# The mixer's u and merge gates z as five steps of seven products, with weight sums in DRAM, and i and v ahead of u

## Chip, cores, metric

The kernel runs on one core of a Trainium2 chip (trn2). The metric is the device time of one execution in microseconds. A core has a matrix engine (TensorE, "PE" in the profile; "PEld" is its loading of weights), VectorE (DVE), ScalarE (ACT), GpSimd (POOL) and SyncE (SP); DMA transfers go through queues that SP (q1 in the profile) and POOL (q0) fill, and are carried out by 16 DMA engines. Matrix products add up in PSUM, which has 8 banks of 128 x 512 f32.

## The reference, cut to what matters

Two layers act on x of 512 tokens x 1024 (ALPHA, BETA and norms as in the code): a feed-forward half step, the mixer, another feed-forward half step, each followed by a layer norm. What this case touches is the mixer's input projection and what uses its parts:

```python
zq, zf, zi, zg, zu, zv, za, zb = jnp.split(x @ w_in, IN_SPLITS, axis=-1)   # 512 each for the first six, 1024 for za and zb
...
o = hgrn2_chunkwise(q, k, i, log_f)                     # 4 heads; normalized per head, times silu(zg)
y_a = o @ w_branch_a
u = jax.nn.gelu(zu)
v = layer_norm(jax.nn.gelu(zv), sg_ln_g, sg_ln_b)
mixed = jnp.einsum('gts,bnsgc->bntgc', ws, v) + sg_bs.T[None, None, :, :, None]
y_b = (u * mixed.reshape(B, T, SG_WIDTH)) @ w_branch_b
y = jax.nn.sigmoid(za) * y_a + jax.nn.sigmoid(zb) * y_b
return y @ w_out
```

All is f32. The inputs x and all weights come from DRAM.

## The kernel before, in words

**Precision.** A product of f32 matrices is made as three passes of a faster type: each operand is split into a high part "h" (an ACT conversion) and a low part "l" (a DVE subtraction, `split`, L125 to L127), and high x high, high x low and low x high are added. The activations x are kept split and transposed as xh and xl: four tiles of 128 features x 2 x 512 tokens. `weights` (L129 to L137) loads a block of 128 x 1024 weights (512 KB) by SP into one of NRAW = 4 raw buffers and splits it into two of NW = 10 tiles, so five blocks can stand ready.

**The blocks of features.** `features` (L790) multiplies one block, 128 output features of all 1024 inputs, by all 512 tokens: `proj` (L147, matmul L155) does 8 k-tiles x 3 passes = 24 matmuls of 512 columns into one bank. So are made f and q (8 blocks), g (4 blocks), u (4 blocks, L1060 to L1063, evicted by ACT with the gelu) and z, that is za and zb (16 blocks, L1109 to L1113, evicted by ACT with the sigmoid).

**Seven products.** i and v are made otherwise, in `two_tokens` (L797): x is cut into halves of the tokens and of the features, the weights likewise, and the four block products of each result are made by seven products (the Strassen-Winograd scheme), whose operands are sums. The sums of x, called s1 to s4, are made and split by `x_sums` (L499) as a side task. The sums of the weights (t13, which holds two, t2 and t4) are made in DRAM by POOL's DMAs, `sums_in_dram` (L294): a copy of one quarter, then a DMA that adds another quarter to it, in the order t13, t2, t4, where each needs the one before. Four steps of w_iv have 8.4 MB of this traffic. The FFN works by seven products too, with 256 columns in each matmul (`seven_pairs` L572, matmul L590), the tokens being cut in two.

**The order of work.** The code is one stream. `Flow` (L50 to L80) is a planner with an estimated clock: `tick` is called after each group of matmuls, adds their estimated time and lets the side task that is due do its next step; `finish` runs a task to its end. A task yields the delay to its next step. SUM_GAP = 7000 ns is the delay between the DMA groups of the sums. In the mixer the stream is: f/q blocks with the sums of x and of w_iv as side tasks (L1034, L1035); g; u; `finish` of both tasks; `two_tokens`; the norm of v (L1075 to L1087, whose scale and shift are in sgp, whose reciprocal root is POOL's `vr`, and whose mixing weights and bias are in cst); z, with two side tasks: `head_out` (L983) of each head in turn, and `spatial` (L1091), the mixing matmuls `mx` and, on DVE, `mv` and the splits `sg`; then the branch projections y and the output projection.

`head_out` makes on PE the transposes `kt`, the state `st`, the outputs `o` (L1009); then ACT squares, DVE sums (`ms`, L1013), POOL makes the reciprocal root `rs` (L186, L187), DVE scales (`on`, L1016), PE transposes back (`ot`, L1021), and DVE and ACT make `ov` and `og`. Every engine carries out its own instructions in their order, so one that waits holds up all behind it.

Of the kernel before, what the change touches and what calls it, by code (L numbers as in the profile page):

```python
# [28 lines left out]
F32 = mybir.dt.float32  # L29
# [6 lines left out]
P = 128  # L36
# [47 lines left out]
def trunk(ctx: ExitStack, tc, x_in, xt_in, w13, w2, w_in, w_iv, w_br, w_out, ln_g, ln_b, lb_in, hgn, sgg, sgb, sgws,  # L84
# [414 lines left out]
    def x_sums(s, gap=X_GAP):  # L499
# [21 lines left out]
        parts("s3")  # L521
        for q in range(2):
            V.tensor_tensor(v["s2"][q], firsts[q], v["s1"][q], op=ALU.subtract)
        yield 0.0, gap
        parts("s2")
        for q in range(2):
            V.tensor_tensor(v["s4"][q], v["s4"][q], v["s2"][q], op=ALU.subtract)
        yield 0.0, gap
        parts("s4")
# [219 lines left out]

    def gates():  # L750
# [28 lines left out]
    def mixer(l, lb, om, first, next_weights):  # L779
# [7 lines left out]
        blk = iter(range(4, 32))  # L787
# [9 lines left out]
        def two_tokens():  # L797
# [3 lines left out]
            for k in ks:  # L801
                for name, q, ts in (("A11", k // 2, lo_t), ("A12", 2 + k // 2, lo_t), ("A22", 2 + k // 2, hi_t)):
                    ops[name, k] = xh[q][:, k % 2, ts], xl[q][:, k % 2, ts]
                for name in ("s1", "s2", "s3", "s4"):
                    ops[name, k] = s[name][0][:, k], s[name][1][:, k]
            s.clear()
# [8 lines left out]
            for ps, p in ((A, P1), (B, P6), (C, P5)):  # L815
                for tt in range(2):
# [3 lines left out]
                    elif ps is B:  # L820
                        V.tensor_tensor(u[:, tt], u[:, tt], B[tt], op=ALU.subtract)
                    else:
                        S.activation(p5[:, tt], C[tt], AF.Copy)
            for k in ks:
                for c in ("A11", "s1", "s2"):
                    del ops[c, k]
# [21 lines left out]


# [133 lines left out]
        def head_out(h):  # L983
# [13 lines left out]
            state = gate[h][:, 0, 0:P]  # L997
# [36 lines left out]
        s_task = flow.add(x_sums(s, 6000.0), 2000.0)  # L1034
        in_dram = flow.add(seven.sums_in_dram(seven.order, 4), 12000.0)  # L1035
# [31 lines left out]
        late.append(flow.add(all_out(), 4000.0))  # L1067
        cst = slot("cst")
# [145 lines left out]
def _layout(x, ffn1_w13, ffn1_w2, ffn2_w13, ffn2_w2, ln_g, ln_b, w_in, hg_lb, hg_norm_g, sg_ln_g, sg_ln_b,  # L1214
# [25 lines left out]
    blocks += [feat(16 + j) for j in range(4)]  # L1240
    blocks += [feat(24 + j) for j in range(16)]
# [4 lines left out]
        "x": c(x), "xt": c(np.asarray(x)[0].T.reshape(4, 2, P, T).transpose(0, 2, 1, 3)).reshape(4, P, D), "w13": w13, "w2": w2, "w_in": np.stack(blocks, 1), "w_iv": quarters(iv, KT // 2),  # L1246
# [12 lines left out]
_INS = ["x", "xt", "w13", "w2", "w_in", "w_iv", "w_br", "w_out", "ln_g", "ln_b", "lb", "hgn", "sgg", "sgb", "sgws",  # L1259
# [26 lines left out]
```

## Time and profile before

| what | value |
|---|---|
| time, median of 3 runs | 2036.38 us (2035.0 to 2036.6) |
| profiled execution, its span | 2033.5 us; the median lies 2.9 us above it |
| TensorE busy | 2022.2 us, 99% |
| VectorE, ScalarE, GpSimd busy | 1639.4 (81%), 996.8 (49%), 370.5 us (18%) |
| mean granted TensorE clock | 0.998 |
| first layer: u starts, i and v start, z starts | 430.1, 453.2, 491.3 us |
| second layer: u starts, i and v start | 1440.7, 1463.8 us |
| matmul of 512 columns, of 256 columns, length | 0.39 to 0.40, 0.28 us |

The rows of a timeline give start, length, engine, line, operation, what is written "<-" what is read, and the number of instructions. Matmuls overlap in the pipeline, so a length is longer than the distance to the next start. A row of waits names the waiting engine, tile and line, then what it waited for, and the total, the number and the longest in us. In groups, "busy us, mean ns" is followed by the idle time ahead of them.

### The profile page before, as it was taken

How to read it: one execution, taken by the hardware profiler on the slowest of the kernel's cores; microseconds unless marked ns; L12 is line 12 of the kernel's file. 1: busy time of each engine (PE TensorE's matmuls, PEld its weight loads, DVE VectorE, ACT ScalarE, POOL GpSimd, SP SyncE). 2: the span in 40 equal slices, each digit the busy share in tenths (PEclk: the TensorE clock that was granted, in tenths of full speed). 3: DMA queues.
4: the chain of work that ended last, by engine and by line, in shares of the span. 5: the costliest groups of instructions: out<-in, count | busy, mean ns of one | idle time of the engine just before them, and what ended most of it. 6: DMA issues, size and time to landing. Idle time of an engine off the chain costs nothing. (4 is left out here: it accounts for less than half of the span.)

```text
span 2033.5 us, 33362 instructions
## 1 busy us (share of the span) xinstructions
PE 2022.2 (99%) x12880; PEld 1840.6 (91%) x12880; DVE 1639.4 (81%) x2453; ACT 996.8 (49%) x1438; POOL 370.5 (18%) x478
## 2 busy tenths in 40 slices
PE   9999999999999999999999999999999999999998
PEld 8999988888888999998899999898888889999986
DVE  8999988956436799999789999889564467999986
ACT  6544665336323554556555456662353235444563
POOL 2322002301000143210132320032010002323101
PEclk9999999999999999999999999999999999999999
DMA  6999777735243289988649997776352433999873
GB/s 233 257 258 238 239 253 238 153 110 181 83 154 115 105 234 241 226 258 269 203 153 271 253 243 242 256 231 137 118 175 83 145 114 113 255 239 230 264 258 129
DMA packets 167550, 404.60 MB, mean 199 GB/s; under 512 B 18880, under 2 KB 19008, under 8 KB 167392
## 3 DMA queue, kind: packets, MB, share of 16 engines
q1 hardware_dynamic: 113472, 261.22, 38.2%
q0 software_dynamic: 53920, 141.26, 29.5%
q8 instruction: 101, 1.65, 0.3%
q14 instruction: 57, 0.47, 0.1%
HBM read 380.38 MB, written 131.07 MB: 252 GB/s over the span
## 5 line engine op out<-in xcount | busy, mean ns | idle before, releaser
L307 POOL DMA_DIRECT2D t<-in_w_dram x176 | 145.5, 901 | 219.5 <-DMA t<-in_w_dram 103.1
L127 DVE TENSOR_TENSOR l_pc<-rc,h_pc 128x1024 fp32r<-128x1024 f32 x80 | 97.8, 1222 | 19.0 <-ACT h_pc L126 19.0
L307 POOL DMA_DIRECT2D t<-t x104 | 56.7, 545 | 288.2 <-DMA t<-in_w_dram 258.6
L155 PE MATMUL z<-xh,h_z 128*128 128x512 f32 x256 | 103.2, 403 | 0.0
L155 PE MATMUL z<-xh,l_z 128*128 128x512 f32 x256 | 99.9, 390 | 0.0
L155 PE MATMUL z<-xl,h_z 128*128 128x512 f32 x256 | 99.9, 390 | 0.0
L127 DVE TENSOR_TENSOR l_pa<-ra,h_pa 128x1024 fp32r<-128x1024 f32 x80 | 97.7, 1221 | 0.0
L126 ACT ACTIVATE h_pc<-rc 128x1024 fp32r<-128x1024 f32 x80 | 84.0, 1050 | 21.0 <-PE fB L590 20.0
L186 POOL TENSOR_SCALAR rstd<-ssq 128x1 f32<-128x1 f32 x24 | 19.3, 803 | 406.8 <-ACT sq L211 406.8
L590 PE MATMUL fA<-xh,h_pc 128*128 128x256 f32 x320 | 90.8, 284 | 0.1
L590 PE MATMUL fC<-xs1h,l_pt 128*128 128x256 f32 x320 | 90.7, 283 | 0.0
L590 PE MATMUL fB<-xs2l,h_pa 128*128 128x256 f32 x320 | 90.7, 283 | 0.0
L590 PE MATMUL fC<-xs1l,h_pt 128*128 128x256 f32 x320 | 90.7, 283 | 0.0
L590 PE MATMUL fB<-xs2h,h_pa 128*128 128x256 f32 x320 | 90.7, 283 | 0.0
L590 PE MATMUL fC<-xs4l,h_pd 128*128 128x256 f32 x320 | 90.7, 283 | 0.0
L590 PE MATMUL fE<-xs3l,h_pb 128*128 128x256 f32 x320 | 90.7, 283 | 0.0
L590 PE MATMUL fB<-xs2h,l_pa 128*128 128x256 f32 x320 | 90.7, 283 | 0.0
L590 PE MATMUL fE<-xh,l_pc 128*128 128x256 f32 x320 | 90.7, 283 | 0.0
L590 PE MATMUL fA<-xh,l_pa 128*128 128x256 f32 x320 | 90.7, 283 | 0.0
L590 PE MATMUL fC<-xs4h,l_pd 128*128 128x256 f32 x320 | 90.7, 283 | 0.0
L590 PE MATMUL fE<-xs3h,l_pb 128*128 128x256 f32 x320 | 90.7, 283 | 0.0
L590 PE MATMUL fC<-xs4h,h_pd 128*128 128x256 f32 x320 | 90.7, 283 | 0.0
(411 smaller groups left out, 7561.6 us busy)
## 6 DMA issues: line engine op xcount, KB each, us to landing
t<-in_w_dram POOLq DMA_DIRECT2D x88, 512.0 KB, 8.8
t<-t POOLq DMA_DIRECT2D x104, 256.0 KB, 5.5
r_d<-t SPq DMA_DIRECT2D x104, 256.0 KB, 4.2
t<-in_w_dram POOLq DMA_DIRECT2D x88, 256.0 KB, 7.1
r_c<-in_w_dram SPq DMA_DIRECT2D x44, 512.0 KB, 4.8
ra<-in_w_dram SPq DMA_DIRECT2D x80, 256.0 KB, 6.0
rb<-in_w_dram SPq DMA_DIRECT2D x80, 256.0 KB, 7.2
rc<-in_w_dram SPq DMA_DIRECT2D x80, 256.0 KB, 7.7
```

Source lines behind the costliest of these rows:

```text
L126: pin(S.activation(hi, src, AF.Copy))
L127: pin(V.tensor_tensor(lo, src, hi.bitcast(F32), op=ALU.subtract))
L155: PE.matmul(ps[:, n0:n0 + n], a[:, cs], m[:, n0:n0 + n], start=(i == 0), stop=(i == 3 * nk - 1))
L186: G.tensor_scalar(r, ssq, inv, eps, op0=ALU.mult, op1=ALU.add)
L307: tc.keep_in_program_order(nc.gpsimd.dma_start(*of(k), **kw))
L590: PE.matmul(ps[:, half[z]], a[:, ms], v, start=start, stop=(m == 3 and i == 2), skip_group_check=not (first and z == 0))
```

## The change

20 blocks of each layer, u's 4 and z's 16, are no longer made by `features`, but as five steps of 4 blocks (512 output features): step 0 is u, steps 1 to 4 are z. `columns` makes one step: seven products, each of a weight block of 128 x 1024 (as many bytes as before) with 24 matmuls of 256 columns (L896 of the changed kernel). The operands on the side of x are A11, s1, s2, s4, s3, A12 and A22, in that order; on the side of the weights four quarters of the step's weights, or sums of them, come one block each. X, C and A are banks in which the products add up as a chain: X takes A11, s2, s3 and A22, so between two of them it is evicted and goes on adding. ACT evicts X, C and X again; DVE adds or subtracts at L910 (C), L913 (X, after s3's product) and L916 (A); ACT applies the gelu or sigmoid. Each step uses seven loaded blocks in place of four, so a layer has 35 in place of 20.

`column_sums` makes the steps' weight sums in DRAM on POOL's queue (L870, tiles `zt_`): for each step t13 (1 MB copied, 1 MB added), t2 and t4 (half a MB copied and added each), 4.2 MB. Those of steps 0 to 2 follow the sums of w_iv in the same side task; those of steps 3 and 4 are a side task of their own, added behind step 0 and finished before step 3. The weights come as a new input w_uz, arranged on the host, and w_in loses these blocks.

i and v now stand directly after g, ahead of u. `x_sums` in the mixer changes the signs of s2 and s4, and no longer splits s3 into tiles of its own: `third` splits it in place into the upper token half of xh and xl of the first half of the features, at the start of `two_tokens`, after g has read them. s1, s2 and s4 stay till the end of z. The head's state moves from a part of `gate` to a part of its k.

```diff
+        def third():
+            for q in range(2):
+                split(xh[q][:, :, hi_t], xl[q][:, :, hi_t], v["s3"][q])
...
-            V.tensor_tensor(v["s2"][q], firsts[q], v["s1"][q], op=ALU.subtract)
+            a, b = (v["s1"][q], firsts[q]) if mixer else (firsts[q], v["s1"][q])
+            V.tensor_tensor(v["s2"][q], a, b, op=ALU.subtract)
...
+                ops["s3", k] = xh[k // 2][:, k % 2, hi_t], xl[k // 2][:, k % 2, hi_t]
+            s["third"]()
...
+        def column_sums(steps):
+
+            w = {k: w_uz[l, k] for k in steps}
+            t13, t2, t4 = zd
+            copies = (lambda k: (t13[k], w[k][:, 0:3:2]), lambda k: (t2[k], t13[k][:, 1]),
+                      lambda k: (t4[k], t2[k]))
+            adds = (lambda k: (t13[k], w[k][:, 1:2].broadcast_to([P, 2, D])), lambda k: (t2[k], w[k][:, 0]),
+                    lambda k: (t4[k], w[k][:, 3]))
+            for copy, add, gap in zip(copies, adds, (1.7, 1.0, 1.0)):
+                for of, kw in ((copy, {}), (add, {"accum_op": ALU.add})):
+                    for k in steps:
+                        tc.keep_in_program_order(nc.gpsimd.dma_start(*of(k), **kw))
+                    yield 0.0, SUM_GAP * gap
+
+        def columns(step, out1, out2, func):
...
+            def product(ps, c, src, first):
+                hi, lo = weights(src, f"c{c}{step}")
+                for z in range(2):
+                    for m in range(4):
+                        ms = slice(z * 512 + m * P, z * 512 + (m + 1) * P)
+                        mh, ml = mov(c, m)
+                        for i, (a, v) in enumerate(((hi, mh), (hi, ml), (lo, mh))):
+                            PE.matmul(ps[:, half[z]], a[:, ms], v, start=first and z == 0 and m == 0 and i == 0,
+                                      stop=(m == 3 and i == 2), skip_group_check=not (first and z == 0))
+                        flow.tick(3 * 120.0)
...
+            product(X, "A11", w[:, 0], True)
+            S.activation(out1[:, :, lo_t], both(X), AF.Copy)
+            product(C, "s1", t13[:, 0], True)
+            S.activation(out2[:, :, hi_t], both(C), AF.Copy)
+            product(X, "s2", t2, False)
+            S.activation(out2[:, :, lo_t], both(X), AF.Copy)
+            product(C, "s4", w[:, 2], False)
+            V.tensor_tensor(out2[:, :, lo_t], both(C), out2[:, :, lo_t], op=ALU.subtract)
+            S.activation(out2[:, :, lo_t], out2[:, :, lo_t], func)
+            product(X, "s3", t13[:, 1], False)
+            V.tensor_tensor(out2[:, :, hi_t], out2[:, :, hi_t], both(X), op=ALU.subtract)
+            S.activation(out2[:, :, hi_t], out2[:, :, hi_t], func)
+            product(A, "A12", w[:, 3], True)
+            V.tensor_tensor(out1[:, :, lo_t], out1[:, :, lo_t], both(A), op=ALU.add)
+            S.activation(out1[:, :, lo_t], out1[:, :, lo_t], func)
+            product(X, "A22", t4, False)
+            S.activation(out1[:, :, hi_t], both(X), func)
...
+        def all_sums():
+            yield from seven.sums_in_dram(seven.order, 4)
+            yield from column_sums((0, 1, 2))
+
+        in_dram = flow.add(all_sums(), 12000.0)
...
-        u = [slot(f"u{i}") for i in range(2)]
-        for j in range(4):
-            ps = features(f"u{j}")
-            S.activation(u[j // 2][:, j % 2, :], ps, AF.Gelu_apprx_tanh)
         flow.finish(s_task)
         flow.finish(in_dram)
         two_tokens()
         late.append(flow.add(all_out(), 4000.0))
+        u = [slot(f"u{i}") for i in range(2)]
+        columns(0, u[0], u[1], AF.Gelu_apprx_tanh)
+        more = flow.add(column_sums((3, 4)), 0.0)
...
-        for br in range(2):
-            for d in range(KT):
-                if d % 2 == 0:
-                    z[br].append(slot(f"z{br}{d}"))
-                S.activation(z[br][d // 2][:, d % 2, :], features(f"z{br}{d}"), AF.Sigmoid)
+        for i in range(4):
+            if i == 2:
+                flow.finish(more)
+            zs = [slot(f"z{i}{j}") for j in range(2)]
+            columns(1 + i, *zs, AF.Sigmoid)
+            z[i // 2] += zs
```

On POOL's queue, before, in the first layer behind the sums of w_iv: the loads of cst and sgp, the v norm's `vr`, then the first head's `rs`.

```order
L1071 DMA cst<-in_sgws_dram 128x512
L1072 DMA cst<-in_sgbs_dram 128x512
L1073 DMA sgp<-in_sgg_dram 128x512
L1074 DMA sgp<-in_sgb_dram 128x512
L186 TENSOR_SCALAR vr<-vq 128x1
L187 TENSOR_TENSOR vr<-vr,mhalf 128x1
```

On the same queue now, from the end of the `vr` to `rs` of head 1: `zt_75` and `zt_76` are t13 of steps 3 and 4.

```order
L186 TENSOR_SCALAR vr<-vq 128x1
L187 TENSOR_TENSOR vr<-vr,mhalf 128x1
L870 DMA zt_75<-in_w_uz_dram 256x1024
L186 TENSOR_SCALAR rs<-ms 128x4
L870 DMA zt_76<-in_w_uz_dram 256x1024
L187 TENSOR_TENSOR rs<-rs,mhalf 128x4
L1146 DMA cst<-in_sgws_dram 128x512
L1147 DMA cst<-in_sgbs_dram 128x512
L1148 DMA sgp<-in_sgg_dram 128x512
L1149 DMA sgp<-in_sgb_dram 128x512
L186 TENSOR_SCALAR rs<-ms 128x4
```

The loads of cst and sgp moved from ahead of the four `vr` to behind them and behind `rs` of head 0, with two of the sums' copies between.

Further on in the same queue now, from `rs` of head 2 to `rs` of head 3 (before, two `rs` stood next to each other): `zt_80` and `zt_81` are t2, `zt_85` and `zt_86` t4 of steps 3 and 4, each first copied, then added to.

```order
L186 TENSOR_SCALAR rs<-ms 128x4
L187 TENSOR_TENSOR rs<-rs,mhalf 128x4
L870 DMA zt_80<-zt_75 128x1024
L870 DMA zt_81<-zt_76 128x1024
L870 DMA zt_80<-in_w_uz_dram 128x1024
L870 DMA zt_81<-in_w_uz_dram 128x1024
L870 DMA zt_85<-zt_80 16x8192
L870 DMA zt_86<-zt_81 16x8192
L186 TENSOR_SCALAR rs<-ms 128x4
L187 TENSOR_TENSOR rs<-rs,mhalf 128x4
L870 DMA zt_85<-in_w_uz_dram 128x1024
L870 DMA zt_86<-in_w_uz_dram 128x1024
```

Six DMAs that each need an earlier one now stand ahead of `rs` of head 3.

On DVE now, near the end of step 2 (the second z step), where that `rs` is read; z_5768 is the step's second output, cC_ and cX_ its banks, l_c the low parts of the weights that come next:

```order
L910 TENSOR_TENSOR z_5768<-cC_5770,z_5768 128x2x256
L127 TENSOR_TENSOR l_cs_6083<-r_cs_6080,h_cs_6082 128x1024
L1084 TENSOR_REDUCE ms<-o 128x4
L1087 TENSOR_TENSOR on<-o_5931,rs 128x512
L913 TENSOR_TENSOR z_5768<-z_5768,cX_5769 128x2x256
L127 TENSOR_TENSOR l_cs_6114<-r_cs_6111,h_cs_6113 128x1024
```

Before, `on` of the last head stood between splits of weights, with no eviction of a bank behind it; now the eviction at L913 is the next instruction.

More of the change, by code (lines that the diff above doesn't have):

```diff
@@ L83, in trunk @@
 @with_exitstack
-def trunk(ctx: ExitStack, tc, x_in, xt_in, w13, w2, w_in, w_iv, w_br, w_out, ln_g, ln_b, lb_in, hgn, sgg, sgb, sgws,
+def trunk(ctx: ExitStack, tc, x_in, xt_in, w13, w2, w_in, w_iv, w_uz, w_br, w_out, ln_g, ln_b, lb_in, hgn, sgg, sgb, sgws,
           sgbs, masks, tril_in, ident_in, out):
@@ L748, in ffn @@
         return seven.run(0.5 / ALPHA, (l, 2 * i), last, by_seven[5:], next_weights)
+    zd = [[dram.tile([P] + d, F32, name=f"z{n}{k}", tag=f"z{n}{k}", bufs=1) for k in range(5)]
+          for n, d in (("t13", [2, D]), ("t2", [D]), ("t4", [D]))]
     def gates():
@@ L785, in mixer @@
         nc.gpsimd.dma_start(hg, hgn[l])
-        blk = iter(range(4, 32))
+        blk = iter(range(4, 12))
         s = {}
@@ L820, in two_tokens @@
                     elif ps is B:
[L821 removed]
+                        V.tensor_tensor(u[:, tt], u[:, tt], B[tt], op=ALU.add)
                     else:
                         S.activation(p5[:, tt], C[tt], AF.Copy)
[L824 to L826 removed]
             it.extend(slot(f"i{i}") for i in range(2))
@@ new lines, in columns, with mov, both @@
+        def columns(step, out1, out2, func):
+            lo_t, hi_t = slice(0, 256), slice(256, 512)
+            half = lo_t, hi_t
+            w = w_uz[l, step]
+            t13, t2, t4 = (v[step] for v in zd)
+            def mov(c, m):
+                if c in s:
+                    return s[c][0][:, m], s[c][1][:, m]
+                q, ts = {"A11": (m // 2, lo_t), "s3": (m // 2, hi_t), "A12": (2 + m // 2, lo_t),
+                         "A22": (2 + m // 2, hi_t)}[c]
+                return xh[q][:, m % 2, ts], xl[q][:, m % 2, ts]
+            X, C, A = (bank(f"c{v}{step}") for v in "XCA")
+            def product(ps, c, src, first):
[8 more added lines that the diff above has]
+                        flow.tick(3 * 120.0)
+            def both(ps):
+                return ps.rearrange("p (z t) -> p z t", z=2)
+            product(X, "A11", w[:, 0], True)
[15 more added lines that the diff above has]
+            S.activation(out1[:, :, hi_t], both(X), func)
@@ L1033, in mixer @@
         need(2, 3)
-        s_task = flow.add(x_sums(s, 6000.0), 2000.0)
-        in_dram = flow.add(seven.sums_in_dram(seven.order, 4), 12000.0)
+        s_task = flow.add(x_sums(s, 6000.0, True), 2000.0)
+        def all_sums():
+            yield from seven.sums_in_dram(seven.order, 4)
+            yield from column_sums((0, 1, 2))
+        in_dram = flow.add(all_sums(), 12000.0)
         for h in range(2):
@@ L1239, in _layout @@
     blocks += [feat(12 + j) for j in range(4)]
-    blocks += [feat(16 + j) for j in range(4)]
-    blocks += [feat(24 + j) for j in range(16)]
+    wq = w.reshape(DEPTH, 2, 4, P, 40, P)
+    uz = []
+    for js in [range(16, 20)] + [range(24 + 4 * i, 28 + 4 * i) for i in range(4)]:
+        v = wq[:, :, :, :, list(js)].reshape(DEPTH, 2, 4, P, 2, 2, P).transpose(0, 1, 4, 3, 5, 2, 6)
+        v = v.reshape(DEPTH, 2, 2, P, D)
+        uz.append(np.stack([v[:, 0, 0], v[:, 0, 1], v[:, 1, 1], v[:, 1, 0]], 2))
     iv = np.concatenate([w[:, :, :, j:j + 4].reshape(DEPTH, D, 512) for j in (8, 20)], -1)
@@ L1245, in _layout @@
     return {
-        "x": c(x), "xt": c(np.asarray(x)[0].T.reshape(4, 2, P, T).transpose(0, 2, 1, 3)).reshape(4, P, D), "w13": w13, "w2": w2, "w_in": np.stack(blocks, 1), "w_iv": quarters(iv, KT // 2),
+        "x": c(x), "xt": c(np.asarray(x)[0].T.reshape(4, 2, P, T).transpose(0, 2, 1, 3)).reshape(4, P, D), "w13": w13, "w2": w2, "w_in": np.stack(blocks, 1), "w_iv": quarters(iv, KT // 2), "w_uz": c(np.stack(uz, 1)),
         "w_br": c(br.transpose(0, 1, 4, 3, 5, 2, 6)).reshape(DEPTH, 2, 4, P, D),
@@ L1256, in _layout @@
     }
-_INS = ["x", "xt", "w13", "w2", "w_in", "w_iv", "w_br", "w_out", "ln_g", "ln_b", "lb", "hgn", "sgg", "sgb", "sgws",
+_INS = ["x", "xt", "w13", "w2", "w_in", "w_iv", "w_uz", "w_br", "w_out", "ln_g", "ln_b", "lb", "hgn", "sgg", "sgb", "sgws",
         "sgbs", "masks", "tril", "ident"]
```

15 lines of the change are left out of this document (9 added, 6 removed).

## Prediction

> **What bounds the kernel now.** I read the page first, its span and busy times.
>
> ```profile
> span 2033.5 us, 33362 instructions
> PE 2022.2 (99%) x12880; PEld 1840.6 (91%) x12880; DVE 1639.4 (81%) x2453; ACT 996.8 (49%) x1438; POOL 370.5 (18%) x478
> ```
>
> TensorE is busy for 99% of the span. Then the waits of PE over the whole execution:
>
> ```profile
> PE idle L1150 <- DVE zero L1147: 1.1, 1, 1.1
> PE pE L366 <- DVE l_d L127: 0.6, 1, 0.6
> PE pb L1179 <- ACT h_b L126: 0.3, 1, 0.3
> ```
>
> That is 2.0 us in all, and none of it in u, the i and v products or z. So the time is what PE executes: the change can win by less matmul time only, and lose by any wait of PE, since there is almost none. What room the others have differs by stage, so the windows come next (busy time of PE, PEld, DVE, ACT and POOL with counts, then granted clock, DMA share and GB/s):
>
> ```profile
> 100.00:200.00 100.00, 100.00 (x835) 100.00 (x835) 92.87 (x108) 48.34 (x62) 27.27 (x38) 1.00 0.95 246
> 360.00:380.00 20.00, 20.00 (x114) 18.10 (x114) 20.00 (x67) 6.42 (x12) 7.86 (x11) 1.00 0.98 183
> 500.00:520.00 20.00, 20.00 (x115) 17.37 (x114) 15.52 (x37) 13.95 (x29) 3.53 (x6) 1.00 0.24 79
> 520.00:540.00 20.00, 20.00 (x107) 17.06 (x106) 9.67 (x21) 7.82 (x18) 1.21 (x2) 1.00 0.25 79
> 560.00:580.00 20.00, 20.00 (x102) 16.91 (x101) 7.14 (x8) 6.14 (x9) 2.31 (x4) 1.00 0.41 131
> ```
>
> The last three rows are the first layer's z stage: DVE from three quarters down to a third busy, the DMA engines to a quarter or little more. From 360 to 380 the sums of w_iv are made, with DMA at 0.98. The first row is the FFN, which multiplies by seven products already: DMA at 0.95, and PE full.
>
> **Matmuls removed and added.** From PE's timeline the first and last of 44 z matmuls of 512 columns without other work between, and of 11 FFN matmuls of 256 columns:
>
> ```profile
> 578.16 0.39 PE L155 MATMUL z<-xh,h_z 128*128 128x512 f32 x1
> ...
> 587.91 0.39 PE L155 MATMUL z<-xl,h_z 128*128 128x512 f32 x1
> 149.73 0.28 PE L590 MATMUL fE<-xh,l_pc 128*128 128x256 f32 x1
> ...
> 150.93 0.28 PE L590 MATMUL fA<-xh,h_pa 128*128 128x256 f32 x1
> ```
>
> Start to start that is 9.75 / 43 = 0.2267 us and 1.20 / 10 = 0.120 us; the window from 100 to 200 gives 100 / 835 = 0.1198 for the second. Four blocks of 24 took 96 x 0.2267 = 21.76 us; a step of 7 x 24 takes 168 x 0.1198 = 20.13 us. That is 1.63 us less, and with five steps in each of two layers **16.3 us less**. Seven products for eight should give an eighth, 2.7 us a step; the rest is lost because two matmuls of 256 columns take 0.2396 us where one of 512 took 0.2267.
>
> The Trainium skill, page "TensorE: Matmul & The Clock Gate", section "Wait — 56ns, not 53.3ns?", puts warm matmuls N / 2.4 GHz plus about 2.5 ns apart, measured at 512 as 215.7 ns. By it a step would save 96 x 215.7 - 168 x 109.2 ns = 2.36 us and ten steps 23.6 us, an estimate from that page. The trace, at a granted clock of 1.00, has 226.7 and 119.8 ns; it does not agree, and it decides.
>
> **When the steps stand.** Three starts on PE in the first layer (first u, first product of i and v, first z):
>
> ```profile
> 430.11 0.40 PE L155 MATMUL u<-xh,h_u 128*128 128x512 f32 x1
> ...
> 453.19 0.39 PE L366 MATMUL iA<-h_b,xh 128*128 128x512 f32 x1
> ...
> 491.27 0.39 PE L155 MATMUL z<-xh,h_z 128*128 128x512 f32 x1
> ```
>
> The i and v products last 38.1 us; u's block stretch 23.1 us, 1.3 of it small matmuls of the heads. Now i and v run from 430.1 to 468.2, u to about 490, and with some 1 us of small matmuls in each, z's steps 1 to 4 start near 490, 511, 532 and 553. A block of weights is used in 2.88 us (24 x 0.1198), where one took 5.44.
>
> **Splits and evictions.** A layer's 20 blocks become 35, each with one ACT conversion and one DVE subtraction. The groups between 500 and 580 us (busy, mean ns):
>
> ```profile
> L127 DVE TENSOR_TENSOR l_z<-r_z,h_z 128x1024 fp32r<-128x1024 f32 x11 | 13.5, 1224 | 16.2 <-ACT h_z L126 16.2
> L126 ACT ACTIVATE h_z<-r_z 128x1024 fp32r<-128x1024 f32 x11 | 11.6, 1056 | 14.2 <-PE z L155 14.1
> L127 DVE TENSOR_TENSOR sg<-mv,sg 128x128 fp32r<-128x128 f32 x16 | 3.8, 286 | 0.4 <-ACT sg L126 0.4
> L1016 DVE TENSOR_TENSOR on<-o,rs 128x512 f32<-128x512 f32 x4 | 2.8, 692 | 5.6 <-POOL rs L187 5.6
> L1086 DVE SCALAR_TENSOR_TENSOR v<-v,vr,sgp 128x512 f32<-128x512 f32 x3 | 2.2, 748 | 0.6 <-POOL vr L187 0.6
> ```
>
> 15 more blocks are 18 us of DVE and 16 us of ACT over some 100 us, and each step has three DVE evictions of about 0.69 us. Where DVE had 5 us free of 20 (500 to 520) that is tight; later it is hidden. Without cover a split holds PE for 1.06 + 1.22 = 2.3 us. The sum fits, so I cost these at nothing by themselves and look where DVE's order makes one late:
>
> - Step 0: a head's transposes `ot` wait for `on`, which follows POOL's `rs` and one queued split: 0 to 1.3 us, taken 0.4.
> - Step 1: the v norm waits for sgp and cst. Their DMAs stood ahead of the v norm's `vr` on POOL and now follow `rs` of head 0:
>
> ```profile
> 480.89 0.54 POOL L1073 DMA_DIRECT2D sgp<-in_sgg_dram  x1 [9.82 <-PE iC L366]
> ...
> 511.31 1.01 POOL L187 TENSOR_TENSOR rs<-rs,mhalf 128x4 f32<-128x4 f32 x1
> sgp<-in_sgg_dram POOLq DMA_DIRECT2D x1, 256.0 KB, 4.4
> ```
>
> `rs` of head 0 came 20 us after the i and v products (511.3 against 491.3), so now near 488; four issues of 0.54 and a landing of 4.4 give 494 to 495. The first mixing matmul behind them can wait: 0 to 2 us, taken 0.6. On DVE's queue the rows from `cst` to the eviction at L913 then hold eight scalings (6.0), nine operations of about 0.69 (6.2), three splits (3.7) and sixteen small ones (4.6): 20.5 us, from 494.5 to 515, or to 510 if what doesn't need sgp comes before it. PE's seventh product needs that eviction near 490 + 6 x 2.88 + small matmuls, 508 to 510: 0 to 6 us, taken 2.0, as the busy window of 500 to 520 already held most of this work beside a full PE.
>
> **The sums in DRAM.** Each step adds 4.2 MB of copies and accumulating adds on POOL's queue. Their price is read from w_iv's sums (8.4 MB): issues on POOL's timeline, the median landing, the queues from 340 to 400; then q1, the loads, in the i and v products (453 to 492); then both queues in the FFN (50 to 200):
>
> ```profile
> 348.92 2.26 POOL L307 DMA_DIRECT2D t<-in_w_iv_dram  x4
> 357.01 2.18 POOL L307 DMA_DIRECT2D t<-in_w_iv_dram  x2 [0.99 <-DMA t<-in_w_iv_dram]
> 380.06 0.56 POOL L307 DMA_DIRECT2D t<-t  x1 [2.62 <-DMA t<-in_w_iv_dram]
> 385.42 3.38 POOL L307 DMA_DIRECT2D t<-in_w_iv_dram  x4 [0.44 <-DMA t<-t]
> t<-in_w_iv_dram POOLq DMA_DIRECT2D x8, 256.0 KB, 6.9
> q0 software_dynamic: 3730, 9.38, 70.7%
> q1 hardware_dynamic: 864, 3.15, 15.6%
> q1 hardware_dynamic: 2466, 6.85, 52.9%
> q0 software_dynamic: 8546, 20.48, 63.9%
> q1 hardware_dynamic: 8899, 16.74, 31.9%
> ```
>
> 8.4 MB took from 348.9 to about 395.7 (385.4 + 3.4 + 6.9), 47 us, beside loads of 15.6%. At that pace the 12.6 MB of steps 0 to 2 take 70 us from 389, to 459. From 430 on loads take 53%, which leaves 0.47 in place of 0.84 and stretches the last 29 us to 52: to 482, with step 0's t4 some 5 us earlier. Its product starts near 485.5, load and split ahead of it take about 7, so it is due near 478. Taken as nothing, 0 to 6 us.
>
> Steps 3 and 4 have 8.4 MB again, in POOL's order around the heads' `rs`. The adds follow `rs` of head 1, due near 500; from adds to t4 copies w_iv's took 380 - 357 = 23 us, so the t4 copies are issued near 523 and `rs` of head 3, which stands behind them, at 524. DVE's `on` waits for that `rs`, ahead of step 2's eviction L913, needed by PE near 529. At w_iv's pace it is 3 us early. But a step's loads are 1.58 us of all DMA engines (0.524 MB at 3.0 us per MB, from 6.85 MB in 52.9% of 39 us) in 2.88 us, 55%; with the same stretch of 1.8 the 23 us are 41 and `rs` is 14 us late. The FFN stands between (sums 63.9% beside loads 31.9%, PE full), and SP may hold four raw blocks ahead. 0 to 14 us, taken 2.4, near the early end, since the FFN row is the nearest.
>
> **The sum.** Stalls 0.4 + 0.6 + 2.0 + 2.4 = 5.4 us a layer, 10.8 in all: 16.3 - 10.8 = 5.5 us less. The profiled span of 2033.5 becomes 2028.0; the median of before, 2036.4, lies 2.9 us above that span for what is around it, so 2030.9, or 2031.
>
> **Rivals.**
> - *All hidden*: the order's lateness is covered, as in the FFN. 2036.4 - 16.3 = 2020. For it: no wait of PE at DMA 0.95. Against: DVE's order behind sgp.
> - *Equal turns*: loads and sums alternate on the DMA engines, so that loads get half where 55% is needed: a step takes 20.1 x 55 / 50, 2 us more, while sums run, some four steps a layer: 16 us back with the small stalls' 5 partly inside. About 2037, no change. For it: the DMA share is 0.98 in w_iv's sums. Against: in the FFN loads got what they needed. The Trainium skill, page "DMA: Bandwidth & Descriptors", section "Queues, rings and completion order", states that each DMA engine takes its queue rows in turn, packet by packet. The FFN's 63.9 against 31.9% are not equal turns, but there loads asked for less.
> - *POOL's chain late* (the other side): the sums of steps 3 and 4 at the stretched pace, `rs` of head 3 behind them, `on`, L913 and the splits behind `on` 14 us late in each layer: 2036.4 - 16.3 + 28 and 6 for the smaller stalls = 2054. It decides once the time from adds to t4 copies passes 28 us. For it: 0.98 of DMA at 15.6% loads. Against: FFN.
>
> **Chances.** My forecast (stalls of 2 to 6 us a layer) 0.45; all hidden 0.17; equal turns, or stalls of 6 to 10 us a layer, 0.18; POOL's chain, at half of its price or more, 0.20. A measurement of this kernel tells about 0.2% from no change, 4 us. Faster by more: 0.62, the first two; within: 0.15; slower: 0.23, with a part of equal turns. The likeliest case alone spans 2024 to 2034. The range takes in all hidden, and POOL's chain up to three quarters of its price (2036.4 - 16.3 + 6 + 21 = 2047): 2018.5 to 2047.
>
> **What would show it.** Right: matmuls of L896 0.12 us apart, ten steps near 20.1 us plus small waits; in PE's waits a few us at cX behind L913 and at `mx`; DMA share 0.9 or more from 390 to 540; t4 copies near 520 to 526. Wrong: waits of PE at L896 behind `l_c` or SP's loads for many us (DMA bound), or `rs` of head 3 far behind its `ms`; or a pace other than 0.12 us, or no waits at all.

## The result and the profile after

The changed kernel takes 2053.53 us (median of four runs, 2051.05 to 2056.06), the kernel before 2035.81 beside it: a ratio of 1.0090, 95% interval 1.0075 to 1.0104. It is slower by 18 us, where 5 us less was forecast, and it lies above the range. The page of the profile after has, for its span and its engines:

```profile
span 2053.5 us, 35115 instructions
PE 2016.8 (98%) x13600; PEld 1871.0 (91%) x13600; DVE 1691.2 (82%) x2513; ACT 1036.2 (50%) x1494; POOL 413.5 (20%) x538
```

PE is busy for 5.4 us less than before, in a span 20 us longer; of the 16.3 us of matmul time that should go, part has come back, and the rest is idle time. PE's waits over the whole execution (total, times, longest):

```profile
PE cC L896 <- ACT z L906: 8.0, 4, 4.1
PE cX L896 <- ACT u L904: 4.5, 2, 2.8
PE mx L1170 <- DVE v L1161: 4.2, 1, 4.2
PE mx L1170 <- issue: 3.6, 1, 3.6
PE cX L896 <- DVE z L913: 2.2, 2, 1.7
...
PE cX L896 <- ACT h_cA L126: 0.9, 1, 0.9
PE cX L896 <- DVE l_cA L127: 0.8, 1, 0.8
PE cC L896 <- ACT u L906: 0.4, 1, 0.4
```

These rows add up to 24.6 us, all in the two mixers: 8.0 at the fourth product of a z step, which waits for an eviction on ACT (L906), 6.6 in u's products, 7.8 at the mixing matmuls `mx`, and 2.2 behind the eviction on DVE at L913. The windows of the first mixer (PE, PEld, DVE, ACT, POOL with counts, granted clock, DMA share, GB/s), of which 500 to 520 and 560 to 580 were shown of before:

```profile
440.00:460.00 20.00, 20.00 (x91) 16.60 (x90) 8.27 (x9) 7.26 (x9) 4.64 (x7) 1.00 1.03 293
480.00:500.00 20.00, 20.00 (x149) 20.00 (x149) 12.26 (x18) 14.56 (x30) 7.90 (x16) 0.86 0.72 239
500.00:520.00 20.00, 16.36 (x126) 16.18 (x126) 11.61 (x16) 6.84 (x10) 4.16 (x4) 0.91 0.49 163
560.00:580.00 20.00, 16.90 (x129) 16.70 (x128) 8.95 (x9) 9.30 (x13) 0.68 (x1) 0.91 0.79 220
```

Before, 480 to 500 had:

```profile
480.00:500.00 20.00, 20.00 (x91) 16.53 (x90) 14.14 (x20) 10.39 (x17) 3.84 (x6) 1.00 0.57 189
```

The DMA engines are full while i and v run, and the granted clock, 1.00 before, is 0.86 and 0.91 in three of the windows. In 480 to 500 PE is busy for all 20 us and yet slow. PE's timeline there:

```profile
479.64 0.58 PE L896 MATMUL cX<-xs2h,h_cs 128*128 128x256 f32 x1 [2.84 <-ACT u L904]
480.02 0.41 PE L896 MATMUL cX<-xs2l,h_cs 128*128 128x256 f32 x1
```

Behind the wait of 2.84 us matmuls start 0.21 us apart, not 0.12, and go on so until 485.8; the granted clock from 480 to 485.8 is 0.50, so this is half clock. The two mixers have five waits of 2.8 us or more (2.84, 3.64 and 3.10; 4.24 and 4.07), and such a stretch stands behind each, mostly 3 to 4 us long; the two of 1.65 and 1.68 us have none. Counted matmul by matmul (0.213 less 0.120 us each), the stretches add 8.2 us over both layers, beyond the waits. Waits and stretches together are 32.8 us; the two mixers, from the end of g to the first y, are 36.6 us longer than the old lengths less the matmul gain, so 3.8 us are not placed.

**Why mx waits.** POOL's queue in the first layer, first copies of the sums of steps 3 and 4, then cst and sgp, then `rs` of head 1, the adds of these sums, and their t4's copy and add:

```profile
490.14 0.65 POOL L870 DMA_DIRECT2D zt<-in_w_uz_dram  x1
...
492.32 0.59 POOL L870 DMA_DIRECT2D zt<-in_w_uz_dram  x1
493.93 0.63 POOL L1146 DMA_DIRECT2D cst<-in_sgws_dram  x1
...
495.62 0.54 POOL L1149 DMA_DIRECT2D sgp<-in_sgb_dram  x1
...
515.76 1.09 POOL L186 TENSOR_SCALAR rs<-ms 128x4 f32<-128x4 f32 x1 [19.60 <-DVE ms L1084]
517.94 2.24 POOL L870 DMA_DIRECT2D zt<-in_w_uz_dram  x2
...
552.14 0.51 POOL L870 DMA_DIRECT2D zt<-zt  x1 [1.95 <-DMA zt<-in_w_uz_dram]
...
555.25 0.91 POOL L870 DMA_DIRECT2D zt<-in_w_uz_dram  x1 [1.22 <-DMA zt<-zt]
```

DVE meanwhile:

```profile
506.92 0.69 DVE L1162 TENSOR_TENSOR cst<-cst,mask 128x512 f32<-128x512 f32 x1 [4.81 <-DMA cst<-in_sgws_dram]
...
509.68 1.42 DVE L1160 SCALAR_TENSOR_TENSOR v<-v,vm,sgp 128x512 f32<-128x512 f32 x2 [2.06 <-DMA sgp<-in_sgg_dram]
...
514.98 0.68 DVE L1084 TENSOR_REDUCE ms<-o 128x4 f32<-128x512 f32 x1
```

The four small loads are issued when the prediction had them, near 494, but land 13 to 14.6 us later, behind two copies of 1 MB on their queue (4.4 us before for the row that the prediction used). That the copies do it is shown by the kernel without the sums of steps 3 and 4 (below): there the four loads are issued at 494.4 to 496.1 and land in 4.1 to 5.5 us. DVE stops for them, so the mixing matmuls wait (in the first layer the profile names no releaser, but the first `v` of L1161 ends just before `mx` starts at 511.86); and `ms` of head 1 stands behind on DVE, so POOL gets `rs` of head 1 at 515.8 and the adds of steps 3 and 4 go at 517.9, not near 500.

**Why L906 waits.** ACT's queue, at u's s2 and at step 3's A22:

```profile
478.05 1.06 ACT L126 ACTIVATE h_cA<-r_cA 128x1024 fp32r<-128x1024 f32 x1 [2.83 <-DMA r_cA<-in_w_uz_dram]
479.01 0.58 ACT L904 ACTIVATE u<-cX 128x512 f32<-128x512 f32 x1
...
569.09 1.06 ACT L126 ACTIVATE h_cA<-r_cA 128x1024 fp32r<-128x1024 f32 x1 [4.68 <-DMA r_cA<-zt]
570.05 0.58 ACT L906 ACTIVATE z<-cC 128x512 f32<-128x512 f32 x1
```

Both times a conversion of later weights waits for its load, 2.83 and 4.68 us, and the eviction that PE wants stands behind it. In the second the load is that of t4 of step 3, whose add was issued at 555.25. So t4 is due three products before its own. SP's queue, which is in order too, brings it forward once more: in the first layer SP stood 9.5 us at the load of t2 of step 3 and 13.0 us at that of t4, issued at 564.35, until their adds had landed, and every later load of weights stood behind them.

**Why u waits.** Landing times and queues between 440 and 475 and, third row, between 488 and 512:

```profile
r_d<-t SPq DMA_DIRECT2D x6, 256.0 KB, 12.5
r_cs<-zt SPq DMA_DIRECT2D x3, 512.0 KB, 12.9
...
sgp<-in_sgg_dram POOLq DMA_DIRECT2D x1, 256.0 KB, 14.6
q0 software_dynamic: 851, 4.19, 50.9%
q1 hardware_dynamic: 1939, 4.95, 39.3%
```

Before, between 440 and 475:

```profile
r_d<-t SPq DMA_DIRECT2D x8, 256.0 KB, 4.1
q0 software_dynamic: 155, 0.51, 4.2%
```

The loads of w_iv's sums (r_d) take 12.5 us now, 4.1 before, when the sums' queue had 4.2% of the engines and not 50.9%. u's first weights are under way beside the last sums as well (r_cs, 12.9 us). The load that ACT waits for at 478.05, A12's, is itself quick: it was issued at 473.66 and landed in 4.4 us. It was issued late, since SP had to wait for DVE to split the slow blocks ahead of it and so free one of the four raw buffers.

### The profile page after: what moved, and what is told of

Same layout as the page of the kernel before. It is cut to its first block, busy times and chain, and to the rows that moved or that the text cites. A ratio compares the mean times of both kernels' runs of the same rounds, so it can differ in the third digit from the quotient of the medians.

```text
span 2053.5 us, 35115 instructions
## 1 busy us (share of the span) xinstructions
PE 2016.8 (98%) x13600; PEld 1871.0 (91%) x13600; DVE 1691.2 (82%) x2513; ACT 1036.2 (50%) x1494; POOL 413.5 (20%) x538
## 5 line engine op out<-in xcount | busy, mean ns | idle before, releaser
L127 DVE TENSOR_TENSOR l_d<-r_d,h_d 128x1024 fp32r<-128x1024 f32 x52 | 63.3, 1223 | 43.7 <-ACT h_d L126 43.5
L598 PE MATMUL fE<-xs3h,h_pb 128*128 128x256 f32 x320 | 90.6, 283 | 0.0
L598 PE MATMUL fA<-xh,l_pc 128*128 128x256 f32 x320 | 90.6, 283 | 0.0
L598 PE MATMUL fE<-xh,h_pc 128*128 128x256 f32 x320 | 90.6, 283 | 0.0
L598 PE MATMUL fA<-xl,h_pa 128*128 128x256 f32 x320 | 90.6, 283 | 0.0
L598 PE MATMUL fC<-xs1h,h_pt 128*128 128x256 f32 x320 | 90.6, 283 | 0.0
```

Of the source, the lines that this page charges most:

```text
L127: pin(V.tensor_tensor(lo, src, hi.bitcast(F32), op=ALU.subtract))
L598: PE.matmul(ps[:, half[z]], a[:, ms], v, start=start, stop=(m == 3 and i == 2), skip_group_check=not (first and z == 0))
```

## The experiments

After the result three causes stood: the sums' copies and adds take DMA time that loads need; the copies hold up small loads and `rs` on POOL's queue; the order on ACT's queue makes one late load stop an eviction. Against them stood the splits and evictions themselves, and the new order of i, v and u. Differences below are differences of ratios times the 2035.8 us of before, since chips differ by a microsecond or two.

**No sums at all.**

```
-            product(C, "s1", t13[:, 0], True)
+            product(C, "s1", w[:, 1], True)
...
-            product(X, "A22", t4, False)
+            product(X, "A22", w[:, 1], False)
-            yield from column_sums((0, 1, 2))
...
-        more = flow.add(column_sums((3, 4)), 0.0)
```

> The changed kernel without any weight sums of the five steps: POOL makes none, and the products s1, s2, s3 and A22 read a quarter of the weights as it stands. Left out: the sums, so u and z are not what the reference has. Both theories: no wait of PE beyond 1 us a layer, and the matmuls' gain of 16.3 us alone, 2018 to 2024 us. Over 2028 us would mean that the evictions or the splits in the order of DVE and ACT cost by themselves, without any late transfer.

2017.23 us, ratio 0.9914 (0.9899 to 0.9928). PE's longest wait:

```profile
PE idle L1223 <- DVE zero L1220: 1.1, 1, 1.1
```

No wait at L896 or `mx`. Its span is 2016.9, 16.6 us below that of before, where the matmul count gave 16.3 (the medians differ by 17.8). So the gain exists, 15 more splits a layer cost nothing, and the sums cost all of the 36 us between this kernel and the changed one.

**The sums made, but not read.** The four product lines as above, the sums kept.

```
-            product(X, "s2", t2, False)
+            product(X, "s2", w[:, 1], False)
...
-            product(X, "A22", t4, False)
+            product(X, "A22", w[:, 1], False)
```

> The changed kernel with all weight sums made as before, but read by nobody: the products s1, s2, s3 and A22 read a quarter of the weights as it stands, so u and z are not what the reference has. The traffic and POOL's queue are the same; no load of SP waits for a sum. Theory 1: the wait at cC behind L906 in step 3 goes with its slow clock (11 us in both layers), those at mx stay: 2040 to 2045 us. Theory 2 (traffic alone): 2048 to 2055 us, with waits of about the same total. If it falls to 2030 or less, the waits for sums held up more than step 3.

2058.18 us, 1.0115 (1.0100 to 1.0130): above what either theory expected.

```profile
PE mx L1170 <- DVE v L1161: 12.9, 2, 6.8
PE cX L896 <- DVE z L913: 10.9, 2, 5.9
PE cX L896 <- ACT u L904: 3.9, 2, 2.1
```

Nothing waits for a sum's value here, yet the sums cost 41 us. The wait behind L906 is gone, which bears out t4's part in it. In its place PE waits at L913, behind `on` and POOL's `rs` of head 3: the chain that the prediction had as its rival on the other side. So the cost doesn't need late sums; what the sums delay is enough. Why `mx` waits longer here than in the changed kernel (12.9 against 7.8 us) stays open.

**The order alone.** In the kernel before, u's loop behind i and v.

```
-        u = [slot(f"u{i}") for i in range(2)]
-        for j in range(4):
...
         late.append(flow.add(all_out(), 4000.0))
+        u = [slot(f"u{i}") for i in range(2)]
+        for j in range(4):
```

> The kernel before with one part of the change alone: i and v ahead of u, all else as before (u by four blocks of 24 matmuls of 512 columns, no sums for u and z). Both theories: the same work moved, no transfer late, 2034 to 2038 us, no change. Over 2040 us would put a part of the loss on the order of i, v and u itself (the v norm on ACT meets u in place of z).

2035.13 us, 1.0001 (0.9991 to 1.0010). The order costs nothing.

**cst and sgp ahead of the copies.**

```
         late.append(flow.add(all_out(), 4000.0))
+        tc.keep_in_program_order(nc.gpsimd.dma_start(wst, sgws[l]))
+        tc.keep_in_program_order(nc.gpsimd.dma_start(bsb, sgbs[l:l + 1, :].broadcast_to([P, 512])))
...
         u = [slot(f"u{i}") for i in range(2)]
         columns(0, u[0], u[1], AF.Gelu_apprx_tanh)
         more = flow.add(column_sums((3, 4)), 0.0)
-        nc.gpsimd.dma_start(wst, sgws[l])
```

> The changed kernel, with the four loads of cst and sgp on POOL's queue directly behind w_iv's and steps 0 to 2's sums, ahead of the v norm's roots and of the copies of steps 3 and 4. Theory 1 (order on POOL's queue: those loads landed 13 to 14.6 us after their issue, behind 2 MB of copies; DVE's queue stood behind them, so heads 1 to 3 and with them the sums of steps 3 and 4 came late): the waits of PE at mx (3.6 and 4.2 us) and most of those at cC behind L906 in step 3 (3.1 and 4.1 us) go, with the slow stretches of the clock behind them: 2053 - 10 - 11, so 2030 to 2036 us. Theory 2 (the 16 DMA engines are full, whatever the order): the waits come back at other loads, 2046 us or more. A middle result, 2040 to 2045, means that mx is cured and step 3 is not.

2039.05 us, 1.0028 (1.0015 to 1.0041).

```profile
PE cX L896 <- ACT u L904: 8.2, 2, 4.3
PE cC L896 <- ACT z L906: 3.0, 2, 2.0
PE ot L1092 <- DVE on L1087: 2.0, 2, 1.0
```

The waits of `mx` are gone, and those behind L906 fall from 8.0 to 3.0, since the sums of steps 3 and 4 go earlier; half clock remains behind u's waits only. Four small loads in another place are worth 13 us of the 18. The result lies between the two theories' ranges: `mx` is cured, but u's waits behind L904 grow from 4.5 to 8.2. The small loads now go beside u's and take 12.8 to 15.2 us themselves; that they are the reason is argued, not shown.

**Which sums cost.** Steps 3 and 4 without sums, then steps 0 to 2 without.

```
+    SUMMED = (0, 1, 2)
...
-            product(X, "s2", t2, False)
+            product(X, "s2", t2 if step in SUMMED else w[:, 1], False)
```

> The changed kernel without the weight sums of steps 3 and 4, whose products s1, s2, s3 and A22 read a quarter as it stands (left out: these sums, so half of z is not the reference's). cst and sgp stay at their place in POOL's order, now with no copy ahead of them. Theory 1: the waits at mx and those of step 3 go, only step 0's stay (6.2 us in both layers and 2.5 us of slow clock): 2026 to 2031 us. Theory 2: half of the traffic gone, a proportional part of the loss back, 2033 to 2038 us.

> The changed kernel without the weight sums of steps 0 to 2, whose products s1, s2, s3 and A22 read a quarter as it stands (left out: these sums, so u and half of z are not the reference's). Theory 1: only step 0's waits go, with their slow clock; cst and sgp still land behind the copies of steps 3 and 4, so mx and step 3 still wait: 2041 to 2047 us. Theory 2: 60% of the traffic gone, 2025 to 2032 us.

2029.69 us, 0.9973 (0.9964 to 0.9983), and 2040.22 us, 1.0029 (1.0017 to 1.0041). Above the kernel with none, 12 us are due to steps 0 to 2 and 23 to steps 3 and 4; together 35, so they add up. Without steps 3 and 4 the largest wait is that of u behind the eviction L904 (L905 there), 4.3 us, and `mx` doesn't wait; without steps 0 to 2:

```profile
PE mx L1170 <- issue: 7.2, 2, 4.3
PE cC L897 <- ACT z L907: 4.5, 4, 2.8
```

u's waits are gone, those at `mx` and behind L906 (L907 there) stay, and the one behind L913 is 4.0 us. So u's waits belong to the sums of steps 0 to 2 and the others to those of steps 3 and 4.

**Evictions ahead of the splits.** Weights are fetched in code order four products ahead, and splits and evictions are kept in that order on ACT and DVE: with cst and sgp early, and in the changed kernel as it is. Since weights are fetched ahead, the sums of steps 3 and 4 are also finished one step sooner in the code.

```
+                fetch(n + AHEAD_C)
+                hi, lo = ready[n]
...
+            tc.keep_in_program_order(S.activation(out2[:, :, hi_t], both(C), AF.Copy))
...
-            if i == 2:
+            if i == 1:
                 flow.finish(more)
```

> e1 (cst and sgp early) with, besides, the order on ACT and DVE held as the code has it: the evictions of a product stand ahead of the split of the block four products later, so that L904 and L906 no longer stand behind the splits of A12's block and of t4. Theory 1 with theory 3 (the evictions are late because ACT's queue waits for a late load ahead of them, which PE itself would need only two or three products later): the waits of e1 at cX behind L904 (8.2 us) and at cC behind L906 (3.0 us) go, with 3.5 us of slow clock: 2039 - 14, so 2023 to 2029 us, faster than before. Theory 2 (the DMA engines are full): PE waits for the same loads a little later, as a wait behind ACT's or DVE's splits, 2035 us or more.

> The changed kernel with the order on ACT and DVE held as in e6, cst and sgp left where they are. Theory 3: the waits at cX behind L904 (4.5 us) and at cC behind L906 (8.4 us) go with their slow stretches (about 5 us); those at mx (7.8 us and 2.5 us of slow clock) stay: 2035 to 2041 us. Theory 1 alone: 2048 us or more, since the sums of steps 3 and 4 are as late as before. Theory 2: 2048 us or more.

2059.80 us, 1.0128 (1.0111 to 1.0145), and 2071.69 us, 1.0178 (1.0163 to 1.0193): both slower than the kernels that they start from. The first one's waits:

```profile
PE cX L909 <- DVE z L928: 13.7, 2, 7.2
PE cX L909 <- DVE l_cA L127: 5.7, 2, 3.4
PE cC L909 <- ACT h_cs L126: 5.0, 2, 3.4
```

Of the waits behind ACT's evictions 2.0 us are left, where the kernel with cst and sgp early had 11.6. But PE waits 13.7 us (21.2 in the second kernel) at the eviction on DVE behind `rs` of head 3 (L928 there, L913 in the changed kernel), and 12.8 us for splits. Two things changed at once, though: with the earlier `finish` that `rs` stands behind the adds of t4 on POOL too (552.5 and 556.5, then `rs` at 557.4; with cst and sgp early alone `rs` came at 544.9, ahead of these adds). So these runs show that this order of ACT's work does not pay as built; what it would be worth by itself stays open.

**Sums in the FFN.** With cst and sgp early: the sums of steps 0 and 1, then 0 to 2, beside the last FFN part ahead of the mixer.

```
+        if i == 0:
+            ahead[:] = [flow.add(column_sums(l, (0, 1)), 0.0)]
...
-            yield from column_sums((0, 1, 2))
+            yield from column_sums(l, (2, 3, 4), 1.5)
```

> e1 with the same sums begun earlier: those of steps 0 and 1 (8.4 MB) on POOL's queue while the FFN ahead of the mixer multiplies by w2, where POOL has nothing and the DMA engines have a share of 0.57 to 0.83; those of steps 2, 3 and 4 behind w_iv's, at one and a half times the delay between their groups. Same traffic, same matmuls, whole computation. Theory 1 (it is lateness: what is queued where, at which time): the rest of e1's waits, 13 us, and its 3.5 us of slow clock go for the most part: 2020 to 2026 us, faster than before. Theory 2 (too much traffic for the engines in all): the waits move into the FFN's loads and the total stays, 2035 us or more.

> As e12, with the sums of steps 0 to 2 (12.6 MB) in the FFN's second part, and only those of steps 3 and 4 behind w_iv's, at the delays of the changed kernel. Theory 1: u's loads meet less traffic than in e12, 2018 to 2024 us, if the 58 us of DMA work still fit under the FFN's loads; if they don't, 2026 us or more, with the waits in the FFN's last part (iE, pE) or at the end of w_iv's sums. Theory 2: 2035 us or more.

2051.99 us, 1.0095 (1.0060 to 1.0130), and 2082.29 us, 1.0233 (1.0218 to 1.0249). Of the first, PE's largest waits:

```profile
PE pA L366 <- DVE l_b L127: 9.8, 6, 4.2
PE pA L366 <- ACT h_b L126: 8.8, 4, 3.8
```

The mixer's steps, from the first cX to the first y, take 117.6 us there (134.5 in the changed kernel, 115.8 without sums); the FFN pays instead, with 18.6 us of waits at its weights, and over twice that with three steps' sums. The kernel before had DMA at 0.55 to 0.83 between 220 and 340 us, where these sums now run, so an average share below 1 did not mean room for 8.4 MB more.

**Only step 0 in the FFN**, begun later, with the sums of steps 1 and 2 at 1.5 times their spacing, and at the old spacing.

```
-            ahead[:] = [flow.add(column_sums(l, (0, 1)), 0.0)]
+            ahead[:] = [flow.add(column_sums(l, (0,), 0.9), 55000.0)]
```

> e1 with the same sums spread thinner: those of step 0 alone (4.2 MB) in the last 60 us of the FFN ahead of the mixer, one DMA at a time, past the stretch in which e12's and e13's FFN waited for its loads; those of steps 1 and 2 behind w_iv's at one and a half times the delays; steps 3 and 4 as in e1. Whole computation. If u's loads are late in e1 because 12.6 MB of sums meet them, the waits at cX behind L904 (8.2 us in e1) fall to about the 3 us of e12, with 3.5 us of slow clock: 2027 to 2032 us, under the kernel before. If the FFN's loads wait again behind step 0's sums, 2033 to 2040 us.

> e14 with the sums of steps 1 and 2 at the delays of the changed kernel, so that they are done before u and stand between no roots of the heads. If the total up to u counts (8.4 MB in place of 12.6 behind w_iv's), the same as e14 or better, 2025 to 2031 us; if the rate counts, u's loads are as late as in e1, 2034 to 2040 us.

2060.02 us, 1.0129 (1.0112 to 1.0145), and 2048.17 us, 1.0067 (1.0051 to 1.0083). Both lie above every range that was expected. With 4.2 MB there PE still waits in the FFN (at pA 8.0 and 8.2 us), and 6.8 and 6.7 us at the mixer's first blocks f, where neither the kernel before nor the changed one waits; the first also waits 11.4 us behind the eviction that is L906 in the changed kernel. POOL issued the first copy at 239 us, since its queue decides when a DMA goes, not the planner's time, so a later start was not tried by this.

**u by plain products.** With cst and sgp early, u by four blocks of 512 columns behind i and v, and no sums for step 0; the sums of steps 3 and 4 begin ahead of u, or behind it. In these two kernels u reads the upper tokens of x after s3 has taken their place, so u is not the reference's; the work is the same.

```
-            yield from column_sums((0, 1, 2))
+            yield from column_sums((1, 2))
...
-        columns(0, u[0], u[1], AF.Gelu_apprx_tanh)
+        for j in range(4):
+            ps = features(f"u{j}")
```

> e1 with u made as before the change (four blocks of 24 matmuls of 512 columns, no sums), still behind i and v; z by four steps as in the change. The sums of steps 1 and 2 (8.4 MB) behind w_iv's, those of steps 3 and 4 begun ahead of u. The matmuls' gain is then 8 x 1.63 = 13.1 us. If the volume of sums ahead of u caused the late loads: no wait in u, and t4 of steps 3 and 4 lands some 20 us earlier than in e1, so 2022 to 2027 us, faster than before. If the DMA engines' total load counts: 2032 us or more.

> e16 with the sums of steps 3 and 4 begun behind u, as in the change. The wait of step 3 behind t4 (3 us and a part of the slow clock in e1) can stay: 2024 to 2030 us by the volume ahead of u, 2032 us or more by the total load.

2039.64 us, 1.0018 (1.0006 to 1.0030), and 2026.50 us, 0.9962 (0.9949 to 0.9975). The second has in PE's waits:

```profile
PE cC L896 <- ACT z L906: 1.6, 2, 0.8
PE cX L896 <- ACT z L904: 1.5, 2, 1.3
```

Four steps by seven products with 16.8 MB of sums a layer cost almost no wait, if some 20 us of plain products lie between i and v and the first step. It is 7.7 us below before by the medians, 9.7 by the profiled spans, of 13.1 that four steps save. The first one's times spread from 2030.4 to 2045.0 us; its profile is of an execution of 2031.7, with one wait of 7.4 us in the heads (st behind ACT's sc), and what makes the others slower is not shown.

**The same with u ahead of i and v**, so that the whole of the reference is computed; with step 3's sums ahead as well in the second.

```
+        u = [slot(f"u{i}") for i in range(2)]
+        for j in range(4):
+            ps = features(f"u{j}")
...
         late.append(flow.add(all_out(), 4000.0))
-        u = [slot(f"u{i}") for i in range(2)]
```

> The whole computation, with u as before the change (four plain blocks, ahead of i and v), z by the change's four steps, sums of steps 1 and 2 (8.4 MB) behind w_iv's, cst and sgp early as in e1, the sums of steps 3 and 4 behind i and v. Matmuls' gain 8 x 1.63 = 13.1 us. If lateness against the first use is what costs: the sums of steps 1 and 2 are done some 30 us ahead of z, waits of 3 us or less a layer, 2021 to 2028 us, faster than the kernel before and the changed one. If the DMA engines' total load counts wherever it lies: 2032 us or more.

> e18 with the sums of steps 1 to 3 (12.6 MB) behind w_iv's and only those of step 4 behind i and v. By the volume that meets the loads of u, i and v: those are late as in the changed kernel's u, with waits in the i and v products, 2028 to 2036 us. By the time at which a sum is needed: t4 of step 3 is no longer late, at most 1 us of waits behind L906, 2020 to 2026 us.

2054.34 us, 1.0093 (1.0079 to 1.0107), and 2034.96 us, 0.9999 (0.9990 to 1.0009). Of the first:

```profile
PE ot L1092 <- DVE on L1087: 12.9, 2, 7.2
PE cC L896 <- ACT z L906: 7.9, 2, 4.2
```

The same matmuls and the same sums as in the kernel just before, and 27 us apart: so it is not the number of bytes that decides. Here `rs` of head 0 stands behind the t13 copies and adds of steps 3 and 4 on POOL and starts at 518.7, while its `ms` was ready at 509.0; in the kernel just before it stands behind one copy. The place of u differs too, so the whole of the 27 us is not shown to be this. With step 4's sums alone beside the heads, 8.9 us of waits at `ot` are left.

**All of z's sums ahead**, in one group and in two.

```
-            yield from column_sums((1, 2, 3))
+            yield from column_sums((1, 2, 3, 4))
...
-        more = flow.add(column_sums((4,)), 0.0)
```

> e19 with the sums of step 4 too behind w_iv's, so that all 16.8 MB stand on POOL's queue ahead of cst, sgp, the v norm's and the heads' roots; whole computation. If only the place on POOL's queue counts: the 8.9 us at ot and the slow clock behind them go, 2019 to 2025 us, faster than the kernel before. If 16.8 MB make the loads of i and v late: waits at iA to iF or in the first z step, 2030 us or more.

> e20 with the sums of steps 1 and 2 finished before those of steps 3 and 4 begin, so that what is needed first is done first and fewer DMAs are under way at once. By the place on POOL's queue the same as e20 or better, 2019 to 2025 us; if the longer chain (six groups more, each after the landing of the one before) runs past i and v, the v norm's roots wait for it and it is 2028 us or more.

2035.30 us, 1.0005 (0.9996 to 1.0014), and 2045.75 us, 1.0053 (1.0041 to 1.0066). No sum is left beside the heads, and still the first only equals the kernel before; in the second, whose chain of sums is longer, `mx` waits 14.8 us behind `v`. The first one's waits of PE:

```profile
PE cX L896 <- ACT z L904: 3.0, 2, 2.1
PE mx L1171 <- DVE v L1162: 2.8, 2, 1.8
PE iE L366 <- DVE l_d L127: 2.6, 4, 0.8
```

These are 8.4 us of the 13.1 that four steps save. Of some 5 us more about 1 is half clock behind the wait of 2.1 us; the rest no run here tells apart. Of all kernels that compute the whole, none beats the one before.

## Why the prediction was wrong

- **Matmuls: right.** 16.3 us from counts and starts; 16.6 without the sums. The step from span to time, taken as 2.9 us, is 1.8 us in the executions here, which is 1 us of the forecast.
- **Order of i, v and u, splits and evictions by themselves: right,** shown by the order alone and by the kernel without sums.
- **The step that failed first: cst and sgp.** The prediction took a landing of 4.4 us from the profile before and a wait of 0.6 us a layer, 0 to 2. The row was true of a queue with no copies ahead; the order quoted with the change shows two copies just ahead. The landing was 13 to 14.6 us (4.1 to 5.5 at the same place without these copies), the wait 3.6 and 4.2 us. The early loads give back 13 us; that is shown. That half of it comes through the late adds of steps 3 and 4 is argued, from the fall at L906.
- **Sums of steps 0 to 2: "taken as nothing, 0 to 6 us".** The working asked when the sums would be there. They were in time, by 469. What cost was the traffic: loads landed in 12.5 us where they took 4.1, and u waited 3.3 us a layer, half clock apart. Taking the sums away ended these waits.
- **t4's due time.** It was put before its own product. ACT's queue puts its conversion ahead of the eviction for the fourth product, three products or 8.6 us sooner: 4.0 us a layer that were not in the sum.
- **DVE behind sgp, 2.0 us a layer, and `on` of step 0, 0.4:** not seen as waits of their own.
- **Price of a wait.** Each was priced at its length. Half clock behind the long ones adds 4.1 us a layer.
- **POOL's chain.** The rival gave 2054, and 2053.5 was measured, but it is not the cause: L913 cost 2.2 us in all, not 28. Its condition held, since from the adds (517.9) to the t4 copies (552.1) 34 us passed, more than 28. But its due time was wrong: PE was to need L913 of step 2 near 529. Without sums, where PE doesn't wait, it needs it at 541.5, since the small matmuls take some 3 us a step and not 1 (115.8 us for five steps, 100.7 of them products); in the changed kernel its earlier waits and slow stretches moved that to 554.9. `rs` of head 3 started at 552.7, so only 0.5 us of wait was left in the first layer. That the two times agree is chance. The chain itself is real: with the sums unread `rs` started at 558.4 and L913 takes 10.9 us, and 13.7 with ACT's order fixed, where `rs` also stands behind two adds more. So the 0.20 stood for a real mechanism, which here came after others and was hardly paid.
- **Equal turns.** It gave 2 us a step while sums run; u waited 3.3 us a layer, so for u something of that size came about. From 440 to 475 the sums had 50.9% of the engines and the loads 39.3%, nearer to halves than the FFN's 63.9 and 31.9%, on which the prediction leaned. The Trainium skill, page "DMA: Bandwidth & Descriptors", section "Queues, rings and completion order", has each engine take its queues in turn, packet by packet. In this window the sums' queue moved 851 packets and the loads' queue 1939, so it doesn't show such turns.

By term and layer the sum was 0.4 + 0.6 + 2.0 + 2.4; it measured 0 + 3.9 + 0 + 1.1, and what it didn't hold was 4.0 (L906), 3.3 (u) and 4.1 (half clock): 16.4 a layer for 5.4. So the steps that failed are these: the landing of cst and sgp was read from a queue without the new sums, the waits behind ACT's evictions and u's late loads were put at nothing, and no wait was given its stretch at half clock.

## What to carry to other kernels

Price a transfer in DRAM by what stands behind it on its queue and beside it on the DMA engines, and take landing times from a stretch that is as full as the one to come. Look for the due time of an operand in the first in-order queue in which something waits for it, not at its own use. Where several small chains share one resource, the first late one is paid and hides the others, so mending it may only show the next.

## What the runs showed of the hardware that was not expected

- A 256 KB load on POOL's queue landed in 14.6 us behind two 1 MB copies, in 4.5 at the same place without them.
- Loads of 256 KB on SP's queue landed in 12.5 us beside sums at 50.9% of the DMA engines, in 4.1 beside 4.2%.
- Half clock (a granted clock of 0.50, matmuls of 256 columns 0.213 us apart) followed each of the changed kernel's waits of PE of 2.84 us or more, mostly for 3 to 4 us, and none of its waits of 1.68 us or less. The length alone does not decide: without the sums of steps 3 and 4 such a stretch began 1 us behind a wait of 2.06 us, and in the kernel with only step 0 in the FFN, at the old spacing, none followed a wait of 3.10 us. The Trainium skill, page "TensorE: Matmul & The Clock Gate", section "What's actually happening", puts the fall to half clock after at least one idle window of about 3.4 us; waits of 2.06 and 2.84 us, shorter than that, were followed by it here, and the measurement decides.
- A few microseconds are enough: with PE at 99% of its span, waits of 24.6 us and their 8.2 us at half clock ate twice the 16.3 us of matmul time that were won.
